# A hybrid decoder layer: GpSimd's split and norm instructions cut to at most 256 columns, and the attention norm of a full head one step later

## The chip, the cores and the metric

The kernel runs on one core of one Trainium2 chip. The metric is the device time of one launch in microseconds. The engines are TensorE (PE, with its weight load PEld), VectorE (DVE), ScalarE (ACT), GpSimd (POOL) and SyncE (SP, which issues DMAs).

## The reference

One layer of a decoder with three kinds of heads side by side, in float32, with 2048 tokens of width 1024:

```python
h = _rms(x, norm_mix_g)
z = h @ w_in + b_in              # q, k, v, f of attention; mLSTM's and HGRN2's columns
qa = _rms(_heads(a_q, 8), a_q_g); ka = _rms(_heads(a_k, 8), a_k_g)
oa = _fox_attention(qa, ka, v, cumsum(log_sigmoid(a_f)))   # causal softmax, decay in the exponent
ob = _mlstm_chunkwise(...)       # 4 heads
oc = _hgrn2_chunkwise(...)       # 4 heads
ya = _rms(_merge(oa), g_a)
yb = sigmoid(b_o) * _rms(_merge(ob), g_b)
yc = silu(c_g) * _rms(_merge(oc), g_c)
x = x + concat([ya, yb, yc]) @ w_out
x = x + _conv_glu(_rms(x, norm_ffn_g), w_up, conv_w, conv_b, w_down)
```

A head has 64 columns; attention has 8 heads, mLSTM and HGRN2 have 4 each.

## The kernel before

**Numbers.** Products keep float32 accuracy through pairs: a matrix is split into a high part `hi` (rounded to the matmul type by a copy on ACT) and the rest `lo`, and PE multiplies `hi·hi`, `hi·lo` and `lo·hi` (`mm3_steps`, L214). Each matrix that PE multiplies in this way costs one subtraction per tile for `lo`, mostly on POOL.

**Stages.** From 0 to about 946 us the projection `z = h @ w_in` and the two recurrent mixers run; from about 946 to 1400 us attention; then the output projection, the norm and the feed-forward layer to the end.

**Projection and mixers.** `load_split` (L195) loads a group of columns of `w_in` in pieces of four row tiles (raw tile 128 x 4 x 256), copies the high part on ACT and subtracts on POOL, two row tiles at a time (128x512). The projection's groups follow; for q and k, `qk_norm_T` multiplies each 128 x 512 tile of z by its reciprocal norm on POOL (L418), PE transposes it (L422), ACT and DVE make the high and low part (L428, L429), and DMAs store them for attention. The mixers `phase_b` (mLSTM) and `phase_c` (HGRN2) run over four blocks of 512 tokens and are interleaved with the projection. HGRN2 doubles its segments in steps: POOL multiplies q by the decays (L736 first, on 64 x 512 for each of two heads; L765 at each doubling, 64 x 256), DVE does k (L766) and the masks (L755), and PE the products (L720, L748). Both mixers end in `finish_heads`: squares, a norm by many 128x16 operations on DVE (L120 to L132, a Newton iteration for the reciprocal root), and a multiplication by the gate on POOL over 128 x 1024 (L676). HGRN2's gate is first multiplied by its gain, also 128 x 1024 on POOL (L807). In this stage a scheduler of the framework lays each engine's instructions in order, from the program's order, its dependences and its own estimates of durations.

**Attention.** The order is written by hand. One step t is one block of 128 keys against 512 queries: scores (`att_scores`, L924 to L927), exponential and high part on ACT (L931, L933), the low part `pl` on POOL in most steps and one step later on DVE in the others (L937), and some steps after that the products with v (`att_values`, L950 to L952). DVE also finds row maxima for a coming head (`att_maxima`, L874 to L895). A head has four query blocks qb of 4, 8, 12 and 16 steps, 40 in all. `Later` is a table of functions to run in later steps: `put(n, f)` runs f at the end of the step n ahead, in the order in which they were put. After a block's last `att_values`, `out` copies the result to SBUF one step on (L958), and `turn` two steps later transposes it on PE into the PSUM tile `k.px` (L964) and copies it into the head's output tile (L967). For heads 0 to 6 `att_finish` then norms the whole head at once: `first`, `square` and `total` in steps 4 to 8, then

```python
    i = 15 if n == 16 else i + 1
    later.put(i, scale)
    for _ in range(4):
        later.put(i, link)
        i += 1
```

`scale` (L1030 to L1032) puts the mean squares into a corner of the same tile `k.px`; each `link` is one part of a Newton iteration there (L981 to L983 in the first, L988 to L990 in the next three, `rms_psum`); four `times` on DVE (L1041), four `gain` on POOL (L1046) and one `store` (L1051) follow in the steps behind. The last head is normed block by block and doesn't pass through the changed branch.

Of the kernel before, what the change touches and what calls it, by code (L numbers as in the profile page):

```python
# [10 lines left out]
F32 = mybir.dt.float32  # L11
# [5 lines left out]
ALU = mybir.AluOpType  # L17
# [4 lines left out]
P = 128  # L22
# [3 lines left out]
HD = 64  # L26
# [151 lines left out]
def load_split(k, wp, src, n=4):  # L178

    nc = k.nc  # L180
    width = src.shape[1]

    k.wn += 1
    at = 64 if k.wn % 2 == 0 and width == 256 else 0
    hi, lo = (
        k.t(wp, [P, 264 * DT], F32R, tag=x)[:, at : at + width * DT].rearrange("p (n c) -> p n c", c=width)
        for x in ("whi", "wlo")
    )
    for q in range(0, DT, n):
        raw = k.t(wp, [P, n, width], tag="wraw")  # L190
        nc.sync.dma_start(raw, src[q * P : (q + n) * P, :].rearrange("(dt p) c -> p dt c", p=P))
        h = hi[:, q : q + n, :]
        nc.scalar.activation(h, raw, AF.Copy)  # L193
        for i in range(0, n, 2):
            nc.gpsimd.tensor_tensor(  # L195
                lo[:, q + i : q + i + 2, :], raw[:, i : i + 2, :], h[:, i : i + 2, :].bitcast(F32), op=ALU.subtract
            )
    return hi, lo


# [207 lines left out]
def qk_norm_T(k, pz, psum, zs, ss, kind, g, store):  # L408

    nc = k.nc  # L410
    rstd = k.t(pz, [P, 16], tag="rstd")
    rms_scale(k, pz, rstd, ss, HD, 1.0, "h")
    gcol = k.gq if kind == "q" else k.gk
    dhi, dlo = (k.s_qh, k.s_ql) if kind == "q" else (k.s_kh, k.s_kl)
    for n, (z, hi, t0) in enumerate(zs):
        z8 = z.rearrange("p tt (h d) -> p (tt h) d", d=HD)
        r8 = rstd[:, 8 * n : 8 * n + 8].unsqueeze(2).broadcast_to([P, 8, HD])
        nc.gpsimd.tensor_tensor(z8, z8, r8, op=ALU.mult)  # L418
        ps = k.t(psum, [P, 2, 2 * P], tag="t", bufs=2)
        for c in range(2):  # L420
            for tt in range(2):
                nc.tensor.transpose(  # L422
                    ps[:, c, tt * P : (tt + 1) * P],
                    z[:, tt, c * P : (c + 1) * P],
                    k.ident,
                )
        lo = k.t(pz, [P, 2, 2 * P], F32R, tag="l", bufs=2)
        nc.scalar.activation(hi, ps, AF.Copy, scale=gcol)  # L428
        nc.vector.scalar_tensor_tensor(lo, ps, gcol, hi.bitcast(F32), op0=ALU.mult, op1=ALU.subtract)  # L429
        for dst, src in ((dhi, hi), (dlo, lo)):  # L430
            store.dma_start(
                dst[g * 256 : (g + 1) * 256, t0 : t0 + 2 * P].rearrange("(c p) t -> p c t", p=P), src.bitcast(F32)
            )
# [228 lines left out]
def finish_heads(k, pb, num, r, gate, epsf, t0, col, sq, out):  # L662

    nc = k.nc
    nc.scalar.activation(sq, num, AF.Square)
    ss = k.t(pb, [P, 16], tag="f_ss")
    nc.vector.tensor_reduce(ss, sq, axis=AX.X, op=ALU.add)
    if r is not None:
        nc.vector.tensor_tensor(ss, ss, r, op=ALU.mult)
        nc.vector.tensor_tensor(ss, ss, r, op=ALU.mult)  # L670
    s = k.t(pb, [P, 16], tag="f_s")
    rms_scale(k, pb, s, ss, HD, epsf, "f")
    if r is not None:
        nc.vector.tensor_tensor(s, s, r, op=ALU.mult)
    nc.vector.tensor_tensor(out, num, s.unsqueeze(2).broadcast_to([P, 16, HD]), op=ALU.mult)
    nc.gpsimd.tensor_tensor(out, out, gate.rearrange("p c (h d) -> p (c h) d", d=HD), op=ALU.mult)  # L676
    nc.gpsimd.dma_start(
        k.s_y[t0 : t0 + BLK, col : col + 256].rearrange("(tt p) c -> p tt c", p=P),
        out.rearrange("p (c h) d -> p c (h d)", h=4),
    )  # L680


def phase_c(k, blk, pb, psum):
    nc = k.nc
# [3 lines left out]
    oc = k.t(pb, [P, 4, 2, 2, HD], tag="p4", bufs=2)  # L688
    for j in range(2):
# [7 lines left out]
            out=kk, in0=th, scalar1=k.lbn[:, j : j + 1], scalar2=k.lbb[:, j : j + 1], op0=ALU.mult, op1=ALU.add  # L697
        )
        tot = k.t(pb, [P, BLK], tag="c", bufs=3)
        nc.vector.tensor_scalar(  # L700
            out=tot, in0=th, scalar1=k.lbb[:, j : j + 1], scalar2=k.lba[:, j : j + 1], op0=ALU.mult, op1=ALU.add
# [5 lines left out]
        q = k.q2  # L707
        att = k.t(pb, [P, 4, 2, P], tag="att")
        engs = (nc.gpsimd, nc.gpsimd, nc.vector)
        heads = [(slice(i * HD, (i + 1) * HD), i) for i in range(2)]  # L710

        def chunks(x):
            return x.rearrange("p (c l) -> p c l", l=P)
# [3 lines left out]
        for c in range(0, 4, 2):  # L717
            ps = k.t(psum, [P, 2, 2, P], tag="b")
            for n in range(2):
# [11 lines left out]
                op=ALU.mult,  # L731
            )

        yield
        for (r, i), eng in zip(heads, engs):
            eng.tensor_tensor(q[r, :, i, :], q[r, :, i, :], chunks(tot[r]), op=ALU.mult)  # L736
        h, lv = 1, 0
        while h < P:

# [61 lines left out]
    for c in range(0, 4, 2):  # L801
# [2 lines left out]
        nc.sync.dma_start(gz, k.s_n[t0 + c * P : t0 + (c + 2) * P, 768:1024].rearrange("(tt p) c -> p tt c", p=P))  # L804
        nc.scalar.activation(gc, gz, AF.Tanh, scale=0.5)
        nc.vector.scalar_tensor_tensor(gc, gc, 1.0, gz, op0=ALU.add, op1=ALU.mult)
    nc.gpsimd.tensor_tensor(gate, gate, k.gbc[:, 256:512].unsqueeze(1).broadcast_to([P, 4, 256]), op=ALU.mult)  # L807
    num = oc.rearrange("p c j i d -> p (c j i) d")
    sq = att.rearrange("p c i (n d) -> p (c i n) d", d=HD)
    finish_heads(k, pb, num, None, gate, 4.0, t0, 768, sq, num)  # L810
# [183 lines left out]
def att_finish(k, st, pa, t0, n, later):  # L994
# [60 lines left out]
    for c in pieces:  # L1055
        later.put(i, lambda c=c: square(c))
        later.put(i + 1, lambda c=c: total(c))
        i += 1
    i = 15 if n == 16 else i + 1
    later.put(i, scale)  # L1060
    for _ in range(4):
        later.put(i, link)
# [838 lines left out]
```

## Time and profile before

| | before |
|---|---|
| time, median of 3 runs | 2910.72 us (2910.49 to 2912.88) |
| profiled execution | 2909.49 us; span 2907.7 us |
| mean granted clock of PE | 0.979 of 2.4 GHz |
| PE busy | 2799.3 us (96%) |
| DVE busy | 1961.4 us (67%) |
| ACT busy | 1278.8 us (44%) |
| POOL busy | 1446.1 us (50%), 1255 instructions |

Busy shares are means over stages with different limits. The span runs from the first to the last instruction; the profiled execution's own time is 1.8 us longer. The clock is the share of full speed that PE was granted: it has two levels, 2.4 GHz (1.0) and 1.2 GHz (0.5), and a stretch's mean tells how much of it was spent at either.

### The profile page before, as it was taken

Reading aid. Unit: us, or ns where it says so; the run is one execution under the profiler, and the core shown is the slowest. Engines: PE = TensorE matmul, PEld = TensorE weight load, DVE = VectorE, ACT = ScalarE, POOL = GpSimd, SP = SyncE. Lnnn points to the kernel's source line nnn. Section 1 sums busy time; section 2 is a strip of 40 time slices with the busy share of each in tenths; the row PEclk is TensorE's granted clock in tenths of the full one; section 3 lists DMA queues with packets and bytes.
Section 4 is the critical chain, followed back from the end, with each engine's and each line's share of the span. In section 5 each row is a group of like instructions: output and inputs, shape, how many; then the busy total and the mean of one; then the engine's idle time right before and its main releaser. Section 6 shows DMA issues by size and latency. Waiting matters only on the chain. (4 is left out here: it accounts for less than half of the span.)

```text
span 2907.7 us, 42807 instructions
## 1 busy us (share of the span) xinstructions
PE 2799.3 (96%) x15053; PEld 2343.7 (81%) x15053; DVE 1961.4 (67%) x3523; ACT 1278.8 (44%) x2167; POOL 1446.1 (50%) x1255
## 2 busy tenths in 40 slices
PE   7999998999998999999999999999999999999999
PEld 7899996989987766666787788888788788888887
DVE  7336787265777767777446577777787577877655
ACT  4224322131322878887423344444455344344443
POOL 2345462344454668776202566666576444444543
PEclk9999997999998999999999999999999999999999
DMA  5434444333225534450456454445778333333766
GB/s 162 127 95 147 137 128 136 101 96 117 90 90 163 120 89 89 95 120 10 135 171 218 149 166 151 158 159 165 248 252 275 98 100 104 109 106 123 238 206 211
DMA packets 346616, 411.06 MB, mean 141 GB/s; under 512 B 47650, under 2 KB 234096, under 8 KB 343232
## 3 DMA queue, kind: packets, MB, share of 16 engines
q1 hardware_dynamic: 292016, 318.45, 37.0%
q10 hardware_dynamic: 51952, 81.45, 7.7%
q0 software_dynamic: 2432, 8.42, 0.8%
q8 instruction: 118, 1.93, 0.3%
q14 instruction: 98, 0.80, 0.1%
HBM read 280.24 MB, written 127.98 MB: 140 GB/s over the span
## 5 line engine op out<-in xcount | busy, mean ns | idle before, releaser
L1297 POOL TENSOR_TENSOR w<-w,w 128x512 fp32r<-128x512 f32 x302 | 404.3, 1352 | 406.0 <-ACT w L1296 334.8
L1485 PE MATMUL ps<-w,w 128*128 128x512 f32 x1848 | 422.6, 390 | 3.6 <-ACT w L1476 1.9
L1485 PEld LDWEIGHTS ps<-w,w 128*128 128x128 f32 x1848 | 347.8, 188 | 77.6 <-ACT w L1476 2.3
L214 PE MATMUL w<-whi,hlo 128*128 128x256 f32 (+1 forms) x1280 | 373.2, 292 | 0.0
L214 PE MATMUL w<-whi,hhi 128*128 128x256 f32 (+1 forms) x1280 | 370.9, 290 | 2.0 <-DVE z L330 2.0
L214 PE MATMUL w<-wlo,hhi 128*128 128x256 f32 (+1 forms) x1280 | 371.8, 291 | 0.0
L937 POOL TENSOR_TENSOR pl<-pf,ph 128x512 fp32r<-128x512 f32 (+2 forms) x240 | 287.9, 1215 | 134.1 <-ACT ph L933 89.7
L1478 POOL TENSOR_TENSOR w<-w,w 128x512 fp32r<-128x512 f32 x154 | 215.3, 1404 | 205.6 <-ACT w L1476 168.3
L1296 ACT ACTIVATE w<-w 128x512 fp32r<-128x512 f32 x302 | 180.2, 627 | 262.8 <-POOL w L1297 83.8
L1477 DVE TENSOR_TENSOR w<-w,w 128x512 fp32r<-128x512 f32 x154 | 180.0, 1177 | 104.8 <-ACT w L1475 102.9
L214 PEld LDWEIGHTS w<-whi,hhi 128*128 128x128 f32 x1280 | 247.3, 193 | 3.7 <-DVE z L330 2.4
L214 PEld LDWEIGHTS w<-wlo,hhi 128*128 128x128 f32 x1280 | 247.4, 193 | 1.6 <-issue 0.2
L214 PEld LDWEIGHTS w<-whi,hlo 128*128 128x128 f32 x1280 | 247.4, 193 | 1.3 <-issue 0.2
L195 POOL TENSOR_TENSOR wlo<-wraw,whi 128x512 fp32r<-128x512 f32 (+1 forms) x112 | 147.8, 1351 | 143.9 <-ACT whi L193 111.4
L931 ACT ACTIVATE pf<-s 128x512 f32<-128x512 f32 (+1 forms) x320 | 172.5, 539 | 81.4 <-PE s L925 40.9
L1302 DVE TENSOR_TENSOR w<-w,w 128x512 f32<-128x512 f32 x176 | 150.9, 876 | 84.3 <-DMA w<-in_w_up_dram 70.0
L933 ACT ACTIVATE ph<-pf 128x512 fp32r<-128x512 f32 (+1 forms) x320 | 185.1, 578 | 10.4
L889 DVE TENSOR_REDUCE mx<-m 128x1 f32<-128x512 f32 x192 | 130.7, 686 | 61.9 <-PE m L874 59.5
L1343 DVE SCALAR_TENSOR_TENSOR u<-ps,fcol,u 128x1023 f32<-128x1023 f32 x88 | 108.9, 1278 | 93.5 <-ACT u L1342 93.5
L1476 ACT ACTIVATE w<-w 128x512 fp32r<-128x512 f32 x154 | 96.6, 628 | 115.5 <-PE ps L1485 90.0
L874 PE MATMUL m<-KB,QB 70*128 70x512 f32 (+2 forms) x320 | 130.6, 418 | 5.6 <-DVE mx L878 5.6
L1475 ACT ACTIVATE w<-w 128x512 fp32r<-128x512 f32 x154 | 95.9, 623 | 89.4 <-POOL w L1478 46.4
(382 smaller groups left out, 7040.6 us busy)
## 6 DMA issues: line engine op xcount, KB each, us to landing
w<-in_w_up_dram SPq DMA_DIRECT2D x182, 256.0 KB
w<-s_g SPq DMA_DIRECT2D x154, 256.0 KB
w<-in_w_down_dram SPq DMA_DIRECT2D x110, 256.0 KB
wraw<-in_w_in_dram SPq DMA_DIRECT2D x48, 512.0 KB
s_g<-u ACTq DMA_DIRECT2D x88, 256.0 KB
w<-s_w SPq DMA_DIRECT2D x88, 256.0 KB
s_g<-w ACTq DMA_DIRECT2D x66, 256.0 KB
x<-in_x_dram SPq DMA_DIRECT2D x32, 512.0 KB
```

Source lines behind the costliest of these rows:

```text
L195: nc.gpsimd.tensor_tensor(lo[:, q + i : q + i + 2, :], raw[:, i : i + 2, :], h[:, i : i + 2, :].bitcast(F32), op=ALU.subtract)
L214: nc.tensor.matmul(out, lsl(lhs[a], i), rsl(rhs[b], i), start=(i == 0 and j == 0), stop=(i == n - 1 and j == 2))
L889: nc.vector.tensor_reduce(mx[:, i, kb : kb + 1], m[:, 0:n], axis=AX.X, op=ALU.max)
L931: nc.scalar.activation(pf[:, c0:], s[:, c0:], AF.Exp)
L933: nc.scalar.activation(ph[:, c0:], pf[:, c0:], AF.Copy)
L937: eng.tensor_tensor(pl[:, c0:], pf[:, c0:], ph[:, c0:].bitcast(F32), op=ALU.subtract)
L1296: nc.scalar.activation(h, t, AF.Copy)
L1297: nc.gpsimd.tensor_tensor(lo, t, h.bitcast(F32), op=ALU.subtract)
L1302: nc.vector.tensor_tensor(t, x, y, op=op)
L1477: nc.vector.tensor_tensor(gl, gr, gh.bitcast(F32), op=ALU.subtract)
L1478: nc.gpsimd.tensor_tensor(wl, wr, wh.bitcast(F32), op=ALU.subtract)
L1485: nc.tensor.matmul(tiles[tile], g[x][:, tile * P : (tile + 1) * P], w[y], start=j == 0 and c == 0, stop=j == nj - 1 and c == 2,)
```

## The change

Five instructions on POOL are cut into pieces of 256 columns: L195 (128x512 into two), L418 (128x512 into two), L676 and L807 (128x1024 into four) and L736 (64x512 into two of 64x256). POOL's instructions of 512 columns in attention (`pl`), L536 and those of the feed-forward layer stay as they are. POOL issues 196 instructions more; every other engine issues as many as before. In attention, the norm of a full head (heads 0 to 6) starts at step 16 instead of 15: `scale`, the four links, times, gains and the store all move one step on.

```diff
--- before.py
+++ after.py
@@ -191,10 +191,9 @@
         nc.sync.dma_start(raw, src[q * P : (q + n) * P, :].rearrange("(dt p) c -> p dt c", p=P))
         h = hi[:, q : q + n, :]
         nc.scalar.activation(h, raw, AF.Copy)
-        for i in range(0, n, 2):
-            nc.gpsimd.tensor_tensor(
-                lo[:, q + i : q + i + 2, :], raw[:, i : i + 2, :], h[:, i : i + 2, :].bitcast(F32), op=ALU.subtract
-            )
+
+        for i in range(n):
+            nc.gpsimd.tensor_tensor(lo[:, q + i, :], raw[:, i, :], h[:, i, :].bitcast(F32), op=ALU.subtract)
     return hi, lo
 
 
@@ -415,7 +414,9 @@
     for n, (z, hi, t0) in enumerate(zs):
         z8 = z.rearrange("p tt (h d) -> p (tt h) d", d=HD)
         r8 = rstd[:, 8 * n : 8 * n + 8].unsqueeze(2).broadcast_to([P, 8, HD])
-        nc.gpsimd.tensor_tensor(z8, z8, r8, op=ALU.mult)
+        for i in range(0, 8, 4):
+            zi = z8[:, i : i + 4, :]
+            nc.gpsimd.tensor_tensor(zi, zi, r8[:, i : i + 4, :], op=ALU.mult)
         ps = k.t(psum, [P, 2, 2 * P], tag="t", bufs=2)
         for c in range(2):
             for tt in range(2):
@@ -673,7 +674,9 @@
     if r is not None:
         nc.vector.tensor_tensor(s, s, r, op=ALU.mult)
     nc.vector.tensor_tensor(out, num, s.unsqueeze(2).broadcast_to([P, 16, HD]), op=ALU.mult)
-    nc.gpsimd.tensor_tensor(out, out, gate.rearrange("p c (h d) -> p (c h) d", d=HD), op=ALU.mult)
+    for c in range(4):
+        oc = out[:, 4 * c : 4 * c + 4, :]
+        nc.gpsimd.tensor_tensor(oc, oc, gate[:, c, :].rearrange("p (h d) -> p h d", d=HD), op=ALU.mult)
     nc.gpsimd.dma_start(
         k.s_y[t0 : t0 + BLK, col : col + 256].rearrange("(tt p) c -> p tt c", p=P),
         out.rearrange("p (c h) d -> p c (h d)", h=4),
@@ -732,8 +735,10 @@
             )
 
         yield
-        for (r, i), eng in zip(heads, engs):
-            eng.tensor_tensor(q[r, :, i, :], q[r, :, i, :], chunks(tot[r]), op=ALU.mult)
+        for r, i in heads:
+            for c in range(0, 4, 2):
+                qi = q[r, c : c + 2, i, :]
+                nc.gpsimd.tensor_tensor(qi, qi, chunks(tot[r])[:, c : c + 2, :], op=ALU.mult)
         h, lv = 1, 0
         while h < P:
 
@@ -804,7 +809,8 @@
         nc.sync.dma_start(gz, k.s_n[t0 + c * P : t0 + (c + 2) * P, 768:1024].rearrange("(tt p) c -> p tt c", p=P))
         nc.scalar.activation(gc, gz, AF.Tanh, scale=0.5)
         nc.vector.scalar_tensor_tensor(gc, gc, 1.0, gz, op0=ALU.add, op1=ALU.mult)
-    nc.gpsimd.tensor_tensor(gate, gate, k.gbc[:, 256:512].unsqueeze(1).broadcast_to([P, 4, 256]), op=ALU.mult)
+    for c in range(4):
+        nc.gpsimd.tensor_tensor(gate[:, c, :], gate[:, c, :], k.gbc[:, 256:512], op=ALU.mult)
     num = oc.rearrange("p c j i d -> p (c j i) d")
     sq = att.rearrange("p c i (n d) -> p (c i n) d", d=HD)
     finish_heads(k, pb, num, None, gate, 4.0, t0, 768, sq, num)
@@ -1056,7 +1062,7 @@
         later.put(i, lambda c=c: square(c))
         later.put(i + 1, lambda c=c: total(c))
         i += 1
-    i = 15 if n == 16 else i + 1
+    i = 16 if n == 16 else i + 1
     later.put(i, scale)
     for _ in range(4):
         later.put(i, link)
```

Line numbers shift: in attention those of the changed kernel are higher by 6.

Three places of the order follow. The first is DVE in attention, in the seventh head, where its query block 1 is turned and the norm of the sixth head begins; `x` is the PSUM tile `k.px`, `ao` a head's output tile, `ass` the sums of squares, `mx` the row maxima. Before:

```order
L895 TENSOR_REDUCE m_2906_14568<-mx_14281 128x4
L1030 RECIPROCAL x_9750<-ao_13701 128x16
L1031 TENSOR_TENSOR ass_2845_14379<-ass_2845_14379,x_9750 128x16
L1032 TENSOR_TENSOR x_9750<-ass_2845_14379,x_9750 128x16
L981 TENSOR_SCALAR x_9750<-x_9750 128x16
L982 TENSOR_SCALAR a16h_14576<-x_9750 128x16
L983 TENSOR_SCALAR x_9750<-x_9750 128x16
L967 COPY ao_14442<-x_9750 128x260
L866 MEMSET mx_14595 128x16
```

With the change:

```order
L901 TENSOR_REDUCE m_2906_14764<-mx_14477 128x4
L973 COPY ao_14638<-x_9946 128x260
L872 MEMSET mx_14783 128x16
L884 ISA m_14785,mx_14783<-m_14785,mnat 128x128
L884 ISA mx_14783 128x1
L1036 RECIPROCAL x_9946<-ao_13897 128x16
L1037 TENSOR_TENSOR ass_2845_14575<-ass_2845_14575,x_9946 128x16
L1038 TENSOR_TENSOR x_9946<-ass_2845_14575,x_9946 128x16
L987 TENSOR_SCALAR x_9946<-x_9946 128x16
L988 TENSOR_SCALAR a16h_14794<-x_9946 128x16
L989 TENSOR_SCALAR x_9946<-x_9946 128x16
```

The six operations of `scale` and of the first link (L1030 to L983, now L1036 to L989) stood ahead of the copy of `turn` (L967, now L973) and now follow it and two operations of the next maxima.

The second is POOL at the end of the projection, where the last q tiles are normed; `h` and `z` are tiles of the projection, `b_qk` mLSTM's output, `s_v`, `s_qh`, `s_ql` and `s_y` buffers in HBM. Before:

```order
L340 MEMSET h_9584 128x4
L342 TENSOR_TENSOR h_9584<-z_9533,h_9584 128x4x64
L345 DMA s_v<-h_9584 128x520
L676 TENSOR_TENSOR b_qk_7318<-b_qk_7318 128x1024
L418 TENSOR_TENSOR z_9386<-z_9386,rstd_9495 128x512
L418 TENSOR_TENSOR z_9441<-z_9441,rstd_9495 128x512
L339 MEMSET h_9590 128x4
L340 MEMSET h_9590 128x4
L342 TENSOR_TENSOR h_9590<-z_9533,h_9590 128x4x64
L677 DMA s_y<-b_qk_7318 128x4x256
L431 DMA s_qh<-h_9438 128x2x256
L345 DMA s_v<-h_9590 128x520
```

With the change:

```order
L338 MEMSET h_9780 128x4
L339 MEMSET h_9780 128x4
L341 TENSOR_TENSOR h_9780<-z_9729,h_9780 128x4x64
L344 DMA s_v<-h_9780 128x520
L419 TENSOR_TENSOR z_9580<-z_9580,rstd_9689 128x256 x2
L419 TENSOR_TENSOR z_9635<-z_9635,rstd_9689 128x256 x2
L338 MEMSET h_9786 128x4
L339 MEMSET h_9786 128x4
L341 TENSOR_TENSOR h_9786<-z_9729,h_9786 128x4x64
L679 TENSOR_TENSOR b_qk_7465<-b_qk_7465 128x256 x4
L344 DMA s_v<-h_9786 128x520
L432 DMA s_qh<-h_9632 128x2x256
```

The multiplications of the norm (L418, now L419) stood behind the 1024-column multiplication by the gate (L676, now L679) and now stand ahead of it; the gate's four pieces follow the next tile of v (L342, now L341).

The third is DVE in the second half of the mixers' second block; `q_94` is HGRN2's q, `nd`, `b_den`, `b_r` and `f_ss` belong to mLSTM's end, `ss`, `hu` and `rstd` to a norm of q or k. Before:

```order
L404 TENSOR_REDUCE ss_4134<-h_4189 128x8
L669 TENSOR_TENSOR f_ss_2564<-f_ss_2564,b_r_2558 128x16
L716 SCALAR_TENSOR_TENSOR q_94<-c_2512,ld_2503 64x4x128 x2
L670 TENSOR_TENSOR f_ss_2564<-f_ss_2564,b_r_2558 128x16
L120 TENSOR_SCALAR hm_4193<-ss_4134 128x16
L121 TENSOR_SCALAR hh_4194<-ss_4134 128x16
L120 TENSOR_SCALAR fm_2569<-f_ss_2564 128x16
```

With the change:

```order
L645 SCALAR_TENSOR_TENSOR b_den_2601<-nd_1853 128x16
L132 SCALAR_TENSOR_TENSOR rstd_4270<-hu_4273,rstd_4270 128x16
L646 TENSOR_TENSOR b_den_2601<-b_den_2601,b_cols_1838 128x16
L130 TENSOR_TENSOR hu_4273<-rstd_4270 128x16
L650 RECIPROCAL b_r_2604<-b_den_2601 128x16
L131 TENSOR_TENSOR hu_4273<-hu_4273,hh_4272 128x16
L132 SCALAR_TENSOR_TENSOR rstd_4270<-hu_4273,rstd_4270 128x16
L668 TENSOR_REDUCE f_ss_2610<-b_qk_1738 128x16
L670 TENSOR_TENSOR f_ss_2610<-f_ss_2610,b_r_2604 128x16
L329 TENSOR_TENSOR z_4310<-w_4311,bias_4159 128x512
L671 TENSOR_TENSOR f_ss_2610<-f_ss_2610,b_r_2604 128x16
L719 SCALAR_TENSOR_TENSOR q_94<-c_2556,ld_2547 64x4x128 x2
```

The q step (L716, now L719) stood ahead of that norm and now stands behind its whole iteration (L130 to L132).

## Rows read from the trace of the kernel before

**Rows 1.** Busy us per stretch: length; PE, PEld, DVE, ACT, POOL (instructions); clock, DMA, GB/s.

```profile
0.00:946.00 946.00, 889.78 (x6281) 822.04 (x6282) 595.87 (x1339) 283.80 (x458) 394.83 (x440) 0.96 0.39 122
425.00:525.00 100.00, 85.36 (x434) 70.84 (x433) 64.87 (x152) 27.84 (x48) 24.32 (x24) 0.83 0.40 126
946.00:1400.00 454.00, 431.42 (x2183) 303.79 (x2182) 335.36 (x844) 372.58 (x705) 325.92 (x281) 0.97 0.40 86
```

**Rows 2.** PE's waits of the whole kernel: total us, times, longest us.

```profile
PE x L964 <- DVE x L983: 13.9, 7, 3.4
...
PE pv L952 <- DVE pl L937: 5.2, 10, 1.0
PE b L573 <- DVE cstate L790: 4.4, 1, 4.4
PE t L422 <- POOL z L418: 4.2, 4, 1.9
...
PE b L621 <- DVE att L727: 3.7, 1, 3.7
PE b L748 <- DVE c L766: 3.6, 2, 2.8
...
PE b L720 <- DVE q L716: 3.1, 1, 3.1
```

**Rows 3.** Timeline around the sixth stall: start, duration, operation [idle before <-releaser].

```profile
1310.95 0.25 DVE L1030 RECIPROCAL x<-ao 128x16 f32<-128x16 f32 x1
...
1312.08 0.18 DVE L983 TENSOR_SCALAR x<-x 128x16 int32<-128x16 int32 x1
...
1312.41 0.44 PE L964 MATMUL x<-ident,oT 65*128 65x65 f32 x4 [1.67 <-DVE x L983]
...
1312.88 0.43 DVE L967 COPY ao<-x 128x260 f32<-128x260 f32 x1 [0.62 <-PE x L964]
```

**Rows 4.** Busy time by stretch, behind the first and the second stall.

```profile
1020.00:1030.00 10.00, 8.34 (x35) 5.42 (x34) 6.08 (x28) 6.07 (x12) 4.14 (x4) 0.83 0.02 5
1080.00:1090.00 10.00, 8.33 (x28) 5.50 (x27) 4.78 (x25) 4.84 (x9) 3.77 (x3) 0.66 0.02 7
```

**Rows 5.** Timeline at the seventh stall.

```profile
1370.43 0.67 PE L964 MATMUL x<-ident,oT 65*128 65x65 f32 x4 [3.42 <-DVE x L983]
```

**Rows 6.** POOL's instructions by line and form: busy us, mean ns | idle before.

```profile
L195 POOL TENSOR_TENSOR wlo<-wraw,whi 128x512 fp32r<-128x512 f32 x96 | 126.8, 1352 | 127.9 <-ACT whi L193 98.2 <-issue 17.4 <-DMA wraw<-in_w_in_dram 10.9
...
L418 POOL TENSOR_TENSOR z<-z,rstd 128x512 f32<-128x512 f32 x32 | 38.5, 1224 | 45.2 <-DVE rstd L132 36.7 <-issue 3.8 <-DVE f_s L674 3.2
...
L342 POOL TENSOR_TENSOR h<-z,h 128x256 fp32r<-128x256 f32 x32 | 26.1, 820 | 29.0 <-ACT h L341 28.7
...
L937 POOL TENSOR_TENSOR pl<-pf,ph 128x256 fp32r<-128x256 f32 x32 | 23.6, 738 | 0.5 <-ACT ph L933 0.3
...
L676 POOL TENSOR_TENSOR b_qk<-b_qk 128x1024 f32<-128x1024 f32 x4 | 9.6, 2391 | 15.5 <-DVE hu L130 8.3 <-DVE b_qk L675 7.1
```

**Rows 7.** Timeline in the projection, 437 to 444, before a wait for DVE.

```profile
437.27 0.17 DVE L132 SCALAR_TENSOR_TENSOR rstd<-hu,rstd 128x16 f32<-128x16 f32 x1
...
438.18 5.94 POOL L195 TENSOR_TENSOR wlo<-wraw,whi 128x512 fp32r<-128x512 f32 x4 [8.77 <-ACT whi L193]
438.36 1.15 DVE L132 SCALAR_TENSOR_TENSOR rstd<-hu,rstd 128x16 f32<-128x16 f32 x1
...
439.43 2.35 DVE L161 SCALAR_TENSOR_TENSOR x<-x,n8r,gmix 128x1024 f32<-128x1024 f32 x1
...
441.70 1.23 DVE L130 TENSOR_TENSOR hu<-rstd 128x16 f32<-128x16 f32 x1
...
443.57 0.41 PE L573 MATMUL b<-ident,b_qk 128*128 128x128 f32 x2 [4.39 <-DVE cstate L790]
```

**Rows 8.** Timeline at the projection's end.

```profile
930.28 0.42 ACT L341 ACTIVATE h<-z 128x256 fp32r<-128x256 f32 x1 [10.36 <-DMA s_v<-h]
...
933.30 1.22 PE L874 MATMUL m<-KB,QB 70*128 70x512 f32 x2 [5.47 <-DVE mx L878]
```

## Prediction, made before the changed kernel was run

> **What bounds the kernel now.** I read the busy time by stretch first. In both stages that the change touches TensorE (PE) works nearly without a pause: 889.8 of the 946 us of projection and mixers, 431.4 of the 454 us of attention [rows 1]. GpSimd (POOL), on which most of the edits lie, is busy for 394.8 of the 946 us. So the time is PE's own work, plus the places where PE waits, plus the stretches in which the granted clock is at 1.2 instead of 2.4 GHz. A longer or shorter POOL instruction counts only through one of the latter two.
>
> Next come PE's waits [rows 2]. The longest entry of the kernel is the transposes of L964, seven times 13.9 us together, each time for VectorE (DVE) at L983. The timeline around one of them shows why [rows 3]. `scale` and the first `link` of the finished head (L1030 to L983, six small DVE operations from 1310.95 to 1312.26) write into the PSUM tile `px`; `turn` transposes the next head's block into the same tile, stands behind them in program order and waits 1.67 us. Steps give the same reading: `att_finish` and that head's last `att_values` run in one step, `scale` falls 15 steps later, and `turn` of query block 1 of the next head falls in that step too, after it. The seventh stall is 3.42 us [rows 5]; the other six make 13.9 − 3.4 = 10.5 us, about 1.7 each.
>
> After some of these stalls PE's clock falls. The 10 us from 1020, which begin with the first stall's end, were granted 0.83, the 10 us from 1080 with the second 0.66 [rows 4]. Full time at 1.2 GHz reads 0.5, so they hold 10 × 0.17 × 2 = 3.4 and 6.8 us at the low level, and half of that is lost: 1.7 and 3.4 us. The fourth stall reads like the first; the third, fifth and sixth show none. Together 6.8 us.
>
> In the projection PE seldom waits for POOL: L422 for L418, four times, 4.2 us [rows 2]. It waits more for DVE: L573, L621, L748 and L720 add up to 4.4 + 3.7 + 3.6 + 3.1 = 14.8 us. What stands behind the first of them is in the timeline [rows 7]: a 128x16 operation, L132, takes 0.17 us at 437.27 and 1.15 us at 438.36, when POOL is in its run of four L195 subtractions (5.94 us); L130, of the same size, takes 1.23 us. Both wait out one POOL instruction, some 1.0 us each, and PE's matmul at 443.57 has then waited 4.39 us.
>
> **The change, part by part.** The profiled execution took 2909.5 us, 1.2 below the median of the three runs; I sum against the former and add 1.2 at the end.
>
> *Step 15 to 16 (seven full heads).* Nothing is added; scale, links, times, gains and store go one step on, and the order now has `turn`'s copy L967 (now L973) ahead of the six operations. Six stalls go: **−10.5**. DVE must still do the six operations, 1.3 us, but now while PE works: DVE sits idle 0.62 us right after the stall [rows 3], and ACT and POOL were held up by the same matmuls. What is late next is the fourth link, three operations of about 0.18 us [rows 3], which comes one step nearer to a `pl` subtraction that DVE does for L952, a wait of 5.2 us in ten places already [rows 2]. Between 0 and 0.55 us a head; I take 0.2, six times: **+1.2**. The gains on POOL also move behind one more `pl`; POOL has 454 − 326 us free in this stage [rows 1], so nothing. The store moves by a step of about 1.4 us and is read long after.
>
> *The seventh head.* Its stall is longer because DVE itself was late, and the six operations explain only 1.3 of the 3.42 us [rows 3, 5]. That lateness stays and meets PE at the next L952. Bounds: 1.3 (only the six) and 3.4; I take 2.5, as ordinary stalls give back all of their 1.7: **−2.5**.
>
> *Clock after the stalls.* 6.8 us are lost behind three of them. If a pause makes the clock fall, no pause keeps it; but three like pauses had no such effect, so the link isn't strict. Bounds 0 and −6.8; I take **−5**.
>
> *GpSimd's cuts: what they cost POOL.* 112 subtractions of L195 become 224; 32 multiplications of L418 become 64; 16 of 64x512 at L736 become 32; eight of L676 and four of L807, of 1024 columns, become 48 pieces. No row has the same lines at 256 columns; the nearest are L937 at 738 ns and L342 at 820 ns [rows 6]. Two of these against one L195 (1352): +0.12 to +0.29 us, 112 times, 14 to 32 us. Against L418 (1224): +0.25 to +0.42, 8 to 13 us. Four against one L676 or L807 (2391): +0.56 to +0.89, twelve times, 7 to 11 us. L736 priced like L195: 2 to 5. In all 31 to 61 us on an engine with 551 idle us in this stage [rows 1], covered by PE's own work. The Trainium skill speaks against such cuts: its page "GPSIMD Engine Reference", section "Elementwise — side-by-side cycle accounting", says that each GpSimd instruction pays a dispatch in software and a join of eight cores. [rows 6] agree (256 columns cost more than half of 512), and were POOL the bound, the sum would come out slower by those 31 to 61 us.
>
> *Where POOL is on the path.* The four waits at L422 get two halves that take 0.25 to 0.42 us longer: +1.2 for the four. Against this, the order puts the last L418 ahead of the 1024-column L676, which it followed, and 1.9 of the 4.2 us was that place [rows 2]: **−1** for both. The pause right behind it, 5.47 us at L874, stays: ACT had waited 10.36 us there for a DMA of s_v, which is issued as early as before [rows 8]. L676 now runs after that wait and pushes POOL's stores of q behind four pieces, about 3 us; the first heads need them only later. Zero, with ±3 for the range.
>
> *What the cuts give DVE.* A blocked operation waits for one piece, and a piece of 0.74 to 0.82 us instead of 1.35 about halves that. In [rows 7] two blocked operations of 1.0 us would save 1 us of the 4.39, a quarter. I take this quarter for all four waits on DVE, 14.8 / 4: **−4**. Bounds: 0 and, with what the clock loses, −22 (below). The Trainium skill, "SBUF — State Buffer", section "Who interferes with whom", calls the port a lock that goes to whoever issues first. By that rule alone a POOL run of pieces could take it again before DVE, the term would be 0 and the time 2893 us; in [rows 7] L132 ends inside the run of four, so DVE does get in between pieces.
>
> Sum: −10.5 + 1.2 − 2.5 − 5 − 1 − 4 = −21.8; 2909.5 − 21.8 + 1.2 = **2889 us**.
>
> **The rivals.**
> *A, slower: a re-laid order.* The cuts change the scheduler's clock, and it lays the whole projection stage anew: one of HGRN2's q steps (L716, now L719) goes behind a whole norm on DVE. The mixers' matmuls in the middle stand 16 to 59 projection matmuls later. The mixers are chains PE-DVE-PE; where the projection's matmuls run out beside them, PE idles. The price of such a stretch is in the trace: 425 to 525 has PE busy 85.4 of 100 us at a clock of 0.83 [rows 1], 14.6 us idle and 100 × 0.17 = 17 us lost at the low clock, 32 in all. One more stretch of that kind gives 2889 + 32 = 2921 us; it turns the sign once more than two thirds of it (22 us) appears. For it: the order changes in many places, and the old one may have been a lucky one. Against it: the work is the same, POOL and DVE only get freer.
>
> *B, no change to speak of: DVE paces attention.* The six operations still lie on a DVE that feeds PE with maxima and `pl`. If only the idle 0.62 us after a stall [rows 3] and a bit, 0.8 of each 1.7 us, is hidden, six heads give 4.9, nothing else comes: 2910.7 − 4.9 = 2906 us. For it: L952 waits for DVE's `pl` ten times already. Against it: DVE is busy only 335 of 454 us [rows 1].
>
> *C, much faster: the DVE-bound stretches open.* If the 14.8 us of waits shrink by two thirds (−10) and a bit over two thirds of the 17 us at the low clock between 425 and 525 goes too (−12), the projection gives −22 instead of −4: 2871 us. For it: every blocked DVE operation in such a stretch is on PE's chain. Against it: most blocked operations are hidden, and the waits for matmuls' results stay.
>
> *D: the change doesn't do what it says.* A turn that still finds `px` occupied by another link would leave the stalls, and only the projection's −5 would come, 2906 us. The order has the copy first, so it's unlikely.
>
> **How the numbers follow.** Forecast 0.60 (by itself 2880 to 2897 us), A 0.07, B 0.11, C 0.18, D 0.04. Leaving out A and the outer parts of B, C and D, the range is 2868 to 2906 us. A measurement of this kernel can tell about 0.2%, 5.8 us, from no change: below 2904.9 lie forecast, C and half of B (0.83); within lie the rest of B and D (0.10); above lies A (0.07).
>
> **What would show it.** The waits of L964 (now L970) for DVE should be gone from PE's list, the clock at 1020 and 1080 near 1.0, and attention some 14 to 18 us shorter; the waits at L952 may grow by 1 to 4 us. POOL's busy time up to 946 should rise by 31 to 61 us while DVE's falls; the 128x16 operations' longest should fall from over 1.1 to about 0.8 us. Wrong would be: attention shorter by under 8 us (B), the projection stage longer by over 15 us, with new waits and a clock under 0.9 between 330 and 525 (A), or shorter by over 15 us (C).

## The result, and the profile after

The changed kernel takes 2882.9 us (median of 4 runs, 2878.6 to 2886.1) against 2911.8 us: 0.9903 of before, 95% interval 0.9888 to 0.9918, or 29 us less. The profiled execution took 2882.4 us, 27.1 less than that of before. I split it at three marks of the trace, the end of the last projection matmul and the first and the last product with v:

| stretch | before | after | difference | forecast |
|---|---|---|---|---|
| start to the projection's end | 923.8 | 915.4 | −8.4 | −4 |
| to the first product with v | 21.9 | 22.7 | +0.8 | −1 |
| to the last product with v (attention) | 462.9 | 441.8 | −21.1 | −16.8 |
| to the end of PE's work | 1493.2 | 1494.4 | +1.2 | 0 |

The waits of PE, to be held against [rows 2] (total us, times, longest):

```profile
PE pv L958 <- DVE pl L943: 9.3, 10, 2.0
...
PE m L880 <- DVE mx L884: 8.5, 2, 8.4
PE t L423 <- POOL z L419: 4.2, 6, 0.9
...
PE b L723 <- DVE q L719: 3.1, 1, 3.1
...
PE b L753 <- DVE c L771: 1.4, 3, 0.9
...
PE b L622 <- DVE att L730: 1.0, 1, 1.0
PE b L574 <- DVE cstate L795: 0.7, 1, 0.7
PE x L970 <- ACT oT L964: 0.7, 1, 0.7
```

The 13.9 us at the head of the list are gone: `turn` (now L970) waits once for ACT and never for the norm. In their place the products with `pl` wait 9.3 us for DVE instead of 5.2. In the projection three of the four waits for DVE of [rows 2] shrank: L573 from 4.4 to 0.7, L621 from 3.7 to 1.0, L748 from 3.6 to 1.4 (now L574, L622, L753); L720 kept its 3.1. PE's wait at L753 for POOL's q grew, from 0.2 to 1.4 us.

Busy time by stretch, as in [rows 1] and [rows 4] (length; PE, PEld, DVE, ACT, POOL; clock; DMA share; GB/s). First the kernel before, up to its projection's end:

```profile
0.00:923.80 923.80, 875.73 (x6237) 812.86 (x6237) 582.07 (x1300) 277.54 (x445) 381.32 (x418) 0.97 0.38 120
```

Then the changed kernel, the last two lines in the stretches behind the first `turn` calls that used to stall:

```profile
0.00:915.40 915.40, 872.81 (x6239) 810.51 (x6240) 559.73 (x1300) 277.17 (x445) 419.99 (x612) 0.98 0.38 121
425.00:525.00 100.00, 85.64 (x428) 71.64 (x427) 66.08 (x157) 27.31 (x48) 28.52 (x48) 0.80 0.39 124
...
938.00:1380.00 442.00, 431.12 (x2230) 306.17 (x2228) 336.99 (x845) 374.22 (x712) 330.73 (x286) 0.99 0.42 90
1010.00:1020.00 10.00, 10.00 (x51) 6.92 (x50) 7.81 (x29) 9.38 (x17) 7.17 (x7) 1.00 0.36 105
1065.00:1075.00 10.00, 10.00 (x51) 6.87 (x50) 7.93 (x29) 9.15 (x17) 7.21 (x6) 1.00 0.33 99
```

Attention runs at a clock of 0.99, behind the places of the stalls at 1.00. The slow stretch from 425 to 525 stayed (0.80, before 0.83). Up to the projection's end DVE is busy 559.7 us where it was 582.1 for the same work, and POOL 420.0 where it was 381.3. Of the 8.4 us that the stretch lost, PE's idle time gives 5.5 (48.1 to 42.6) and its busy time 2.9.

POOL's prices, against [rows 6]:

```profile
L196 POOL TENSOR_TENSOR wlo<-wraw,whi 128x256 fp32r<-128x256 f32 x192 | 148.7, 811 | 88.4 <-ACT whi L193 61.2 <-DMA wraw<-in_w_in_dram 11.0 <-DMA s_kl<-l 8.5
...
L419 POOL TENSOR_TENSOR z<-z,rstd 128x256 f32<-128x256 f32 x64 | 42.3, 692 | 63.3 <-DVE rstd L132 48.5 <-ACT b_qk L666 10.2 <-issue 4.6
...
L741 POOL TENSOR_TENSOR q<-q,c 64x256 f32<-64x256 f32 x32 | 26.0, 814 | 78.2 <-PE b L723 76.5
...
L813 POOL TENSOR_TENSOR p<-p,gbc 128x256 f32<-128x256 f32 x16 | 14.4, 917 | 6.7 <-issue 3.4 <-DVE p L811 3.2
...
L679 POOL TENSOR_TENSOR b_qk<-b_qk 128x256 f32<-128x256 f32 x16 | 11.3, 737 | 12.3 <-DVE b_qk L676 5.9 <-DVE hu L130 4.4 <-DVE hm L120 2.0
```

Two pieces of L195 take 2 × 811 − 1352 = 0.27 us more than one long instruction, within the forecast's 0.12 to 0.29; L418's only 2 × 692 − 1224 = 0.16, and four of L807 (now L813) 4 × 917 − 2399 = 1.27, more than the 0.56 to 0.89 of the forecast.

### The profile page after: what moved, and what is told of

Its sections match the earlier page's. It is cut to its first block, busy times and chain, and to the rows that moved or that the text cites. A ratio compares the mean times of both kernels' runs of the same rounds, so it can differ in the third digit from the quotient of the medians.

```text
span 2880.2 us, 42984 instructions
## 1 busy us (share of the span) xinstructions
PE 2791.3 (97%) x15053; PEld 2339.8 (81%) x15053; DVE 1934.2 (67%) x3523; ACT 1277.4 (44%) x2167; POOL 1486.3 (52%) x1451
## 5 line engine op out<-in xcount | busy, mean ns | idle before, releaser
L196 POOL TENSOR_TENSOR wlo<-wraw,whi 128x256 fp32r<-128x256 f32 (+1 forms) x224 | 172.1, 805 | 105.8 <-ACT whi L193 78.6
```

What stands on the lines that cost most here:

```text
L196: nc.gpsimd.tensor_tensor(lo[:, q + i, :], raw[:, i, :], h[:, i, :].bitcast(F32), op=ALU.subtract)
```

## The experiments

The attention part was read almost directly from the trace. What stayed open was the projection: the cuts also make the scheduler lay every engine anew, so its −8.4 us could come from shorter waits of DVE (first theory) or from a new order that happens to be better (second theory). One table holds the kernels below; all columns behind the ratio are from one profile each. Six kernels or repeats have the change's projection, with PE's matmuls in the same order: the change twice, the cuts alone, and the three in which only multiplications in attention are moved as well. They ended the projection at 913.0 to 920.2 us, 915.8 in the mean, and the two with the old projection, before and the step alone, at 924.2 in the mean. So the cuts' 8 us are clear of the spread, but a difference under some 7 us between two single profiles says nothing alone. DVE is its busy time over the whole kernel. The last two columns are PE's waits up to the projection's end, summed from the wait list by the engine that ended them; what that engine itself had waited for isn't told by the sum.

| kernel | time, median | ratio to before | projection's end | attention | DVE | PE waits for DVE | for POOL |
|---|---|---|---|---|---|---|---|
| before | | | 923.8 | 462.9 | 1961.4 | 42.1 | 2.7 |
| the change | 2882.9 | 0.9903 (0.9888 to 0.9918) | 915.4 | 441.8 | 1934.2 | 33.9 | 5.6 |
| the change, again | 2883.2 | 0.9890 (0.9871 to 0.9910) | 920.2 | 441.8 | 1936.4 | 35.0 | 6.2 |
| step alone | 2891.7 | 0.9924 (0.9908 to 0.9940) | 924.5 | 443.0 | 1954.7 | 44.1 | 2.7 |
| cuts alone | 2902.3 | 0.9961 (0.9947 to 0.9974) | 915.2 | 462.4 | 1935.1 | 35.7 | 6.2 |
| step, cut of L195 | 2893.6 | 0.9927 (0.9911 to 0.9942) | 931.6 | 443.4 | 1933.7 | 35.9 | 10.7 |
| step, the other four cuts | 2884.2 | 0.9897 (0.9880 to 0.9915) | 915.7 | 441.8 | 1941.2 | 38.0 | 2.9 |
| long instructions, new order | 2899.1 | 0.9951 (0.9934 to 0.9967) | 930.2 | 441.8 | 1954.9 | 43.4 | 7.6 |
| cut instructions, old order | 2881.6 | 0.9901 (0.9877 to 0.9925) | 917.9 | 442.8 | 1939.3 | 38.3 | 3.7 |
| cut of L195, old order | 2888.1 (one run) | | 924.2 | 441.7 | 1946.2 | 39.6 | 3.0 |
| the other four cuts, old order | 2887.2 (one run) | | 921.4 | 443.5 | 1943.2 | 40.4 | 3.0 |
| change, times every 2nd step | 2877.0 | 0.9879 (0.9857 to 0.9901) | 913.0 | 437.1 | 1931.5 | 32.6 | 6.1 |
| the same, again | 2882.9 | 0.9884 (0.9864 to 0.9904) | 916.5 | 436.9 | 1929.5 | 32.5 | 6.1 |
| change, times 3 steps later | 2878.9 | 0.9882 (0.9865 to 0.9899) | 914.5 | 438.5 | 1936.1 | 32.1 | 5.4 |

Each ratio is to runs of the kernel before on the same chip. The chips differ (medians of before 2911.8 to 2915.8 us), so between kernels the ratios are compared rather than the times.

**The step alone.** The kernel before with this line:

```diff
-    i = 15 if n == 16 else i + 1
+    i = 16 if n == 16 else i + 1
```

> The kernel before with the step alone (norm of a full head at step 16, no GpSimd instruction cut). Own theory: the two parts add up and the step acts in attention only; the seven waits of the transposes and the clock behind them go, attention gets 21 us shorter as with the whole change (first product with v to the last, 462.9 us before), projection and mixers stay as before to within 1 us; time -20 (-17 to -22). Rival 'the cuts help attention too' (through a shorter POOL start or the clock they hand over): attention shorter by 10 to 15 us only, time -12 to -15.

Attention fell by 19.9 us and the projection stayed (924.5). The step is worth 0.9924, 22 us by the times, three quarters of the whole.

**The cuts alone** (the rest of the diff, `i = 15`).

> The five cuts alone, the norm still at step 15. Own theory (DVE waits out shorter POOL instructions): DVE's busy time up to the end of the projection falls by some 20 us as with the whole change, the projection ends 8 us earlier, attention keeps its seven waits and its half-clock stretches; time -8 (-5 to -11). Rival 'a new order, by luck': it ends the projection as early too, since the order is the same one; this run alone doesn't tell the two apart, it prices the part. Rival 'cuts cost': +0 to +5, if the projection's gain needs something of the step.

The projection ended at 915.2, attention kept its waits to the digit:

```profile
PE x L969 <- DVE x L988: 13.9, 7, 3.4
```

The two parts add up within the noise: 0.9924 × 0.9961 = 0.9885, within the interval of the second measurement of the change and just below that of the first (0.9888 to 0.9918).

**Which cut.** The step with the cut of L195 alone, and the step with the other four.

> The step and the cut of L195 alone (L418, L676, L736 and L807 uncut). Own theory: L195 stands behind nearly half of DVE's blocked time, so it gives half or more of the cuts' part: DVE's busy time in the projection falls by 10 to 15 us, the projection ends 4 to 8 us earlier than before, time -25 (-22 to -28). Rival 'a new order, by luck': the scheduler lays a third order, and the projection's end lies anywhere within 10 us of that before, on either side, without following DVE's busy time.

> The step and the cuts of L418, L676, L736 and L807, L195 uncut. Own theory: a quarter of DVE's blocked time stands behind these four; DVE's busy time in the projection falls by 5 to 8 us, the projection ends 1 to 4 us earlier than before, time -22 (-20 to -25). Rival 'a new order, by luck': the projection's end within 10 us of that before on either side, without following DVE's busy time; a gain as large as the whole change's, or a loss of over 2 us, would speak for it.

Here the first theory got into trouble. With L195 alone DVE's busy time fell by 21.0 us against the step's, as far as with all five cuts, and the time didn't move (0.9927 against 0.9924). The four others freed 13.5 us of DVE and gave everything. The profile of the L195 kernel shows a loss elsewhere: from 425 to 525 the clock fell to 0.74, and PE was busy 4 us less there than with the step alone or the whole change (85.6 each).

```profile
425.00:525.00 100.00, 81.25 (x370) 65.42 (x370) 62.43 (x149) 27.30 (x48) 21.48 (x28) 0.74 0.37 118
```

What took the gain away stands in the last two columns: PE's waits for DVE did fall, from 44.1 to 35.9 us, but those for POOL rose from 2.7 to 10.7, most of it at the transposes behind the norm of q and k (here L416 and L420, in both kernels uncut):

```profile
PE t L420 <- POOL z L416: 8.8, 6, 5.2
```

At the longest of them POOL itself had waited for DVE's norm:

```profile
476.35 1.04 POOL L416 TENSOR_TENSOR z<-z,rstd 128x512 f32<-128x512 f32 x1 [11.12 <-DVE rstd L132]
```

So where the scheduler puts things seems to matter too, and free runs mix the two. They had to be taken apart.

**Order held, length changed.** Each instruction of the projection stage is chained to its predecessor on its engine in a given order (`LAID`, a table of 285 to 5629 places per engine). In this part of the edit `t` is one engine's table, packed, and `log` the stage's instructions of that engine in program order.

```diff
+            at = np.frombuffer(zlib.decompress(base64.b64decode(t)), np.int16)
+            for x, y in zip(at[:-1], at[1:]):
+                tc.add_manual_dep(
+                    log[y],
+                    log[x].name,
+                    mybir.DependencyInfo(mybir.DependencyClass.NoSync, mybir.DependencyReason.DATA),
+                    reason="order",
+                )
```

One kernel has the long instructions in the change's order, which is held on PE, DVE, ACT and SP while POOL's own order is left to the scheduler; one has the cut instructions in the order of before, held on all five engines. Both have the step.

> The step with all of GpSimd's instructions long as before, but the projection's instructions on TensorE, VectorE, ScalarE and SyncE held, one by one, in the order that the scheduler laid for the changed kernel (GpSimd's own order left to the scheduler). First theory (shorter waits of DVE for POOL): the projection ends where it did before the change, 922 to 925 us, and the time is that of the step alone, about 2891. Second theory (the new order): the projection ends at 914 to 918 us although DVE's busy time stays 10 us or more above the changed kernel's, time about 2883.

> The whole change, with all its cut instructions, but the projection's instructions on all five engines held in the order of before (a long instruction's pieces in its place). First theory (shorter waits of DVE for POOL): DVE's busy time falls by some 20 us and the projection ends at 914 to 918 us, time about 2883. Second theory (the new order): DVE's busy time falls as much, but the projection ends at 920 to 925 us, time 2888 to 2892.

| ratio (projection's end; PE's waits for DVE) | long | cut |
|---|---|---|
| old order | 0.9924 (924.5; 44.1) | 0.9901 (917.9; 38.3) |
| new order | 0.9951 (930.2; 43.4) | 0.9903 (915.4; 33.9) |

The new order with long instructions is slower than with cut ones by 14 us, and the intervals (0.9934 to 0.9967 against 0.9888 to 0.9918) lie apart: the second theory falls, the order of the four engines by itself gives nothing. That it ended even later than the first theory expected (922 to 925 us) stays open: PE's waits for DVE are those of the old order, those for POOL are higher (7.6 us), and POOL's order wasn't held. Two of its waits, which with the change are 1.0 (L622) and 1.6 us (L784):

```profile
PE b L632 <- DVE att L738: 3.9, 1, 3.9
...
PE b L790 <- DVE bstate L641: 3.1, 1, 3.1
```

In the old order the cuts gave some 7 us by the ratios and 6.6 us by the projection's end; there the intervals overlap, and the gain rests on the waits. PE's matmuls stand in the same order in the step alone and in this kernel, so they can be laid side by side one by one: PE's pauses are 6.8 us shorter in all, 2.3 of it at L621, 1.6 at L573, 1.6 at L748 and 0.8 at L783, all waits for DVE. (Of these L748 is unsure: in the two profiles without a cut its waits read 3.6 and 5.1 us.) How it works can be read off. This is the stretch of [rows 7] in the kernel with cut instructions and old order (its lines are 12 to 17 higher):

```profile
436.52 0.16 DVE L144 SCALAR_TENSOR_TENSOR rstd<-hu,rstd 128x16 f32<-128x16 f32 x1
...
437.56 5.13 POOL L208 TENSOR_TENSOR wlo<-wraw,whi 128x256 fp32r<-128x256 f32 x6 [9.44 <-ACT whi L205]
437.61 0.71 DVE L144 SCALAR_TENSOR_TENSOR rstd<-hu,rstd 128x16 f32<-128x16 f32 x1
438.24 1.81 DVE L173 SCALAR_TENSOR_TENSOR x<-x,n8r,gmix 128x1024 f32<-128x1024 f32 x1
439.97 0.69 DVE L142 TENSOR_TENSOR hu<-rstd 128x16 f32<-128x16 f32 x1
...
441.30 0.56 PE L586 MATMUL b<-ident,b_qk 128*128 128x128 f32 x2 [2.88 <-DVE cstate L807]
```

The three DVE operations take 0.71, 1.81 and 0.69 us where they took 1.15, 2.35 and 1.23, together 1.52 us less, and PE's wait behind them is 2.88 us where it was 4.39: 1.51 less. The second such place is the wait of L621, 3.67 us before. There a Newton iteration of `finish_heads` runs beside L195 and then beside L736. Before:

```profile
780.64 5.42 POOL L195 TENSOR_TENSOR wlo<-wraw,whi 128x512 fp32r<-128x512 f32 x4 [9.70 <-ACT whi L193]
...
783.46 1.25 DVE L130 TENSOR_TENSOR fu<-f_s 128x16 f32<-128x16 f32 x1
...
784.84 1.26 DVE L131 TENSOR_TENSOR fu<-fu,fh 128x16 f32<-128x16 f32 x1
786.03 2.65 POOL L736 TENSOR_TENSOR q<-q,c 64x512 f32<-64x512 f32 x2
786.13 1.21 DVE L132 SCALAR_TENSOR_TENSOR f_s<-fu,f_s 128x16 f32<-128x16 f32 x1
787.37 0.18 DVE L130 TENSOR_TENSOR fu<-f_s 128x16 f32<-128x16 f32 x1
...
790.68 0.49 PE L621 MATMUL b<-v,p 128*128 128x130 f32 x2 [3.67 <-DVE att L727]
```

With cut instructions in the same order:

```profile
778.91 6.37 POOL L208 TENSOR_TENSOR wlo<-wraw,whi 128x256 fp32r<-128x256 f32 x8 [8.43 <-ACT whi L205]
...
780.57 0.69 DVE L142 TENSOR_TENSOR fu<-f_s 128x16 f32<-128x16 f32 x1
...
781.39 0.69 DVE L143 TENSOR_TENSOR fu<-fu,fh 128x16 f32<-128x16 f32 x1
782.12 0.66 DVE L144 SCALAR_TENSOR_TENSOR f_s<-fu,f_s 128x16 f32<-128x16 f32 x1
...
782.81 0.66 DVE L142 TENSOR_TENSOR fu<-f_s 128x16 f32<-128x16 f32 x1
...
786.68 0.49 PE L634 MATMUL b<-v,p 128*128 128x130 f32 x2 [1.40 <-DVE att L742]
```

Each of the three is some 0.55 us shorter, POOL's run is one us longer, and PE waits 2.3 us less. Shorter is not fewer: the next two operations of the iteration, which took 0.18 and 0.16 us, now take 0.66 and 0.70. In the changed kernel 45 of the 216 operations of such iterations take over 0.4 us, before 28 did.

One place goes against the rule that a wait lasts one piece. It is the same in all six profiles with the change's projection, where the operation takes 2.95 to 2.98 us; here the changed kernel:

```profile
883.33 2.81 POOL L679 TENSOR_TENSOR p<-p,p 128x256 f32<-128x256 f32 x4
883.91 2.97 DVE L132 SCALAR_TENSOR_TENSOR rstd<-hu,rstd 128x16 f32<-128x16 f32 x1
...
886.18 0.67 POOL L341 TENSOR_TENSOR h<-z,h 128x256 fp32r<-128x256 f32 x1
```

DVE's operation begins inside the first of four pieces and ends only behind all four and the subtraction after them (L341), where an uncut L676 had held up an operation for 2.19 us. PE has no wait in the next 10 us. Why DVE got in between pieces elsewhere and not here isn't shown.

**The cuts' shares in the old order.** The same chain, with the cut of L195 alone and with the other four.

> The step and the cut of L195 alone, the projection's instructions on all five engines held in the order of before (the two pieces in the long one's place). If shorter waits of DVE for POOL give the gain and the scheduler's third order cost the 7.8 us in the free run with this cut: the projection ends at 919 to 922 us, 3 to 5 us before the step's 924.5, DVE's busy time 6 to 12 us under the step's. If cutting L195 itself costs (POOL's longer time, later low parts): it ends at 926 us or later.

> The step and the cuts of L418, L676, L736 and L807, L195 uncut, the projection's instructions held in the order of before. If the shares follow DVE's blocked time (L195 42 of some 65 us): the projection ends at 922 to 924 us, 1 to 3 us before the step's 924.5, and the free run's 915.7 owed some 6 us to its order. If these four stand where DVE is on PE's path: 918 to 920 us.

The projection ended 0.3 and 3.1 us earlier than with the step alone, together 3.4, with all five 6.6; within the spread of single profiles that settles nothing, and the 3 to 5 us expected of L195 weren't seen. The waits tell more: PE's for DVE fell from 44.1 us to 39.6 with the cut of L195, to 40.4 with the other four and to 38.3 with all. So both take part, and in the old order L195's cut doesn't bring the waits for POOL of the free run (3.0 against 10.7). How much time each is worth stays open.

**The new waits in attention.** On top of the change, the four multiplications at every second step, or three steps later:

```diff
-        i += 1
+        i += 2 if n == 16 else 1
```

> The whole change, with the four multiplications (times, each with its gain one step on) of a full head's norm at every second step, 20, 22, 24 and 26, instead of 20 to 23. If the new waits of 0.93 us at L958 in six heads come from the three multiplications and the link that DVE does ahead of that low part: they fall to the 0.3 us of before or less, attention 3 to 5 us shorter, time -3 to -5 against the change. If DVE is late there for another reason (maxima, rows of maxima): no change within 1 us in attention.

> The whole change, with the four multiplications of a full head's norm three steps later, at 23 to 26, each with its gain one step on. If the new waits at L958 come from the multiplications ahead of that low part: the waits fall to 0.3 us or less as in the run with every second step, unless the next low part on DVE, four steps later, meets them and waits instead (0.5 us or more, no gain). If from another reason: no change within 1 us in attention.

> The changed kernel as it is, on the same chip as the next one: time 0.9903 of before (0.989 to 0.992).

> The whole change with the four multiplications at every second step, again, beside the change on one chip: attention 4.7 us shorter than the change's, 437 against 442 us from the first to the last product with v; time 4 to 6 us under the change's. If the earlier difference in the times was one of chips: attention still 4.7 us shorter, the medians within 2 us.

Attention became 4.7 and 4.9 us shorter at every second step, and the waits at L958, 9.3 and 1.3 us with the change (8.3 and 1.3 in its second profile), fell in both profiles (the first, then the second):

```profile
PE pv L958 <- DVE pl L943: 5.1, 10, 2.0
PE pv L958 <- POOL pl L943: 0.6, 1, 0.6
```

```profile
PE pv L958 <- DVE pl L943: 5.2, 10, 2.0
PE pv L958 <- POOL pl L943: 0.6, 1, 0.6
```

The timed runs on one chip don't tell the two kernels apart (0.9884 against 0.9890), so whether this version beats the change stays open. Three steps later gave 3.3 us in attention; its waits moved to POOL's `pl` (3.2 us in eight places).

## Why the prediction was right

It gave 2889 us and a range of 2868 to 2906; measured 2882.9, 6 us less. Attention gave 4.3 us more than its terms and the projection 4.4 more, the boundary 1.8 and the rest 1.2 less.

- **Six stalls, −10.5.** As forecast: none is left, and with the step alone attention already has its 443 us. The steps' reading (same step, earlier in the table, same PSUM tile) was the whole mechanism.
- **The next thing late, +1.2.** The right place, too small, and for another reason: PE now waits some 0.93 us in each of six heads at one L958. The fourth link, which the sum had named, is over 3.6 us before that `pl` begins; three multiplications and a step of the row maxima (L908) stand right ahead of it on DVE, as in the second head, and with the multiplications spread out the wait falls to some 0.25 us.

```profile
1079.78 0.41 DVE L1047 TENSOR_TENSOR asq<-ao,x 128x256 f32<-128x256 f32 x1
1080.22 0.68 DVE L908 TENSOR_TENSOR QB<-m,ident 4x512 fp32r<-4x512 f32 x1
1080.94 0.85 DVE L943 TENSOR_TENSOR pl<-pf,ph 128x256 fp32r<-128x256 f32 x1
...
1081.84 0.33 PE L958 MATMUL pv<-pl,V 128*65 128x256 f32 x1 [0.96 <-DVE pl L943]
```

  In two heads it replaced longer waits, so all waits for `pl`, DVE's and POOL's, grew from 5.2 [rows 2] and 3.3 to 9.3 and 1.3 us, by 2.1.
- **The clock after the stalls, −5.** All of it came: the granted clock reads 1.00 at the old places, and heads that had lost time to a low clock fell from 59 to 55 us, those without from 55.7 to 54.5. That is the 6.8 us read behind them. How much there is to get is in part luck: with the cuts alone the same seven waits stand, and the clock reads 0.83 behind five of the first six and 1.00 behind the second, where before it was 0.66.
- **The seventh head, −2.5.** It fell from 61.5 to 57.0 us with the change and to 59.4 with the step alone, 2.1 to 4.5. The part above the bound of 3.4 is the clock again, which the sum had left out here: it read 0.71 in the 10 us behind that stall before (3 us lost), and the change's first profile has no low clock in this head.
- **POOL's longer work, 0.** Busy up to the projection's end rose by 38.7 us, within 31 to 61. It wasn't quite free: PE's waits for POOL in the projection grew from 2.7 us to 5.4 to 6.2 in the six profiles, less than those for DVE fell. So the warning of the Trainium skill ("GPSIMD Engine Reference", "Elementwise — side-by-side cycle accounting") holds for POOL's time, two pieces cost more than one, and not for the kernel's, in which POOL isn't the bound.
- **L422 and the boundary, −1.** Missed by 1.8 us. Its longest wait did fall from 1.9 to 0.9 us, but its total stayed 4.2 us, and the pause behind grew from 5.47 to 8.37 us: PE only came to it earlier, as ACT's wait for s_v decides when it ends: PE goes on 3.0 us behind that ACT operation, before [rows 8] and now.

```profile
922.02 0.42 ACT L340 ACTIVATE h<-z 128x256 fp32r<-128x256 f32 x1 [11.14 <-DMA s_v<-h]
...
925.05 1.22 PE L880 MATMUL m<-KB,QB 70*128 70x512 f32 x2 [8.37 <-DVE mx L884]
```

- **What the cuts give DVE, −4.** The mechanism was right in the main and the size too small: the stretch became 8.4 us shorter (4 to 11 in the six profiles, against the old mean of 924.2). The step took a quarter of 14.8 us, worked out from one wait in which two blocked operations would save 1 us. In the old order that wait fell by a third (1.5 us: a third, long operation was blocked too, which the sum had left out) and L621's by 62%. The rule in the Trainium skill, "SBUF — State Buffer", "Who interferes with whom", that the port goes to whoever issues first, could have let POOL's next piece shut DVE out. The rows above show both: DVE operations ending one after another inside a single POOL run, so that a shorter piece does shorten the wait, and one of 2.97 us that was shut out for a whole run.

Of the rivals, A (a re-laid order costs) may be real in kind: with long instructions the new order is 8 us slower by the ratios, but the intervals just overlap and POOL's order wasn't held; the cut of L195 in its own order gave nothing. In the change it was more than paid for. B fell with attention's 21 us. C came by half: the four waits fell from 14.8 to 6.2 us, of which other, new waits took a part back, and the low clock between 425 and 525 stayed. D fell with the waits of L970 for DVE.

## What to carry to other kernels

Where a small operation of one chain stands ahead of another chain's in the program and both use one tile, the later chain waits for the whole run. Here a step's delay of the chain that has time cost 2 us and saved 14, and the pauses that went took stretches at the low clock with them. Long instructions of an engine with time to spare can still hold the bound, through operations of a third engine that wait for them to end. And when an edit makes a scheduler lay the program anew, hold the order fixed on every engine and change the length alone, and the reverse, before crediting either; waits summed by the engine that ends them tell more than the ends of single profiles.

## What was not expected

- Freed time of DVE is a poor measure of the gain: its busy time fell by 21 us with the cut of L195 alone, and the kernel's time didn't change, as PE waited 8 us less for DVE and 8 us more for POOL.
- The longest 128x16 operation should have fallen to about 0.8 us. It rose, from 2.19 us (L131) to the 2.97 of L132 above; the longest L131 now takes 1.13. L771, with a longest of 2.32 us before, is down to 0.97.

```profile
L771 DVE TENSOR_TENSOR c<-c,c_t x48: 398/434/970, 136.5 to 839.9; 128x256 f32<-128x256 f32 x48
```

- One and the same kernel ended its projection at 915.4 and at 920.2 us in two profiles. The gap opens in small steps: the same matmul starts 1.7 us later at 423, 3.1 us later at 639 and 4.6 us later at 835.
